# Prompt attention of a hybrid decoder step: a third PSUM bank for the transposes of the probabilities, and the next head's preparation emitted one step earlier with its factor chain in two parts

## The chip, the cores and the metric

One core of a Trainium2 chip runs the whole program. TensorE (PE) multiplies and transposes into PSUM, which has eight banks of 512 fp32 columns; VectorE (DVE), ScalarE (ACT) and GpSimd (POOL) do the rest, and SyncE (SP) issues nearly all transfers. The metric is the device time of one execution in microseconds, the median of several runs; lower is better.

## The reference, cut to what matters

One inference step of a two-layer decoder for a prompt of 1024 tokens and eight samples. Layer 1 is multi-head latent attention with eight heads; the change touches only its prompt half:

```
def mla_attend_prompt(q_abs, q_pe, ckv, kpe, ks):
    for qb in range(t // Q_BLOCK):                      # 8 blocks of 128 queries
        lo, hi = qb * Q_BLOCK, (qb + 1) * Q_BLOCK
        s = mla_scores(q_abs[:, lo:hi], q_pe[:, lo:hi], ckv[:, :hi], kpe[:, :hi], ks[:, :hi])
        p = jax.nn.softmax(jnp.where(mask[None, None], s, -jnp.inf), axis=-1)
        outs.append(jnp.einsum('bhqk,bkc->bqhc', p.astype(ckv.dtype), ckv[:, :hi]))
...
    ms = (sum(k_nope ** 2) + sum(kpe_raw ** 2)) / QK_HEAD
    kscale = lax.rsqrt(ms + EPS)                        # one factor per key and head
    qn = rms_norm(q, q_g)                               # one factor per query and head
```

## The kernel before

The program is a chain of stages; most of its 2 ms go to the projections, the samples' attention over a paged cache and the two output projections. The prompt's attention, `mla()`, begins when all earlier stages have been emitted and is followed by the output projection `out1()`. fp32 products are made of three matmuls on split operands (`mm3`, lines 189 to 191), of a high part H and a low part L.

`mla()` loops over eight heads `h` and in each over eight blocks `i` of 128 queries. One step (h, i) emits, in this order:

- `soft(h, i)`: scores (matmuls of lines 1421 to 1427 into one or two banks of the pool `mm`, which has three), a multiply with a running maximum on DVE (`ass`, line 1429), the negated maximum (`anb`, 1432), the exponential on ACT (1434), the reciprocal of its sum on DVE (`als`, 1435);
- in even heads from 2 on, at i = 2 to 5, one tile of the values for two heads (`vals`, 12 matmuls of 256 columns, here called a values tile);
- one part of the generator `prep(h + 1)`, which prepares the next head: two halves of the keys (k c0, k c1), two of the queries (q c0, q c1), the sums of squares (`ast`, line 1366, copied by DVE to `asts`, 1368), their transposes (line 1372) with the factor chain on DVE (lines 1376 to 1379, where `rsqrt_` makes ten small instructions on 128x16 elements), and last the transpose `tk` (1382) and the stores and loads of the key factor;
- `step(h, i - 2)`: the transposes of the probabilities of two blocks earlier (`tr`, line 1453, tile `atp`, one bank for up to four 128x128 transposes), then, after each second block, the product with the values (`pvl`, tile `aO`), then the split of the transposed probabilities into `aPTH` (ACT, line 183) and `aPTL` (DVE, line 179), which frees the bank.

Of PSUM's eight banks `mm` has three, tag `s` two, and tags `x`, `v` and `t` one each. `atp` rotates through the two of `s`; `ast`, `ast2` and `tk` use `v`, `aO` uses `t`; `x` serves stages before `mla()` and is not used in it.

All engines run their instructions in order. The order on each engine follows the program, but the layer below moves instructions of one engine past each other where it reckons that they would wait, so the emitted order is read from the listing of each engine.

`prep` is advanced once before the loop over i and once in each step:

```
g0 = prep(0)
for _ in range(5):
    next(g0)
...
for h in range(8):
    nxt = prep(h + 1) if h < 7 else iter(())
    ...
    next(nxt, None)
    for i in range(8):
        ss, ls = soft(h, i)
        ...
        next(nxt, None)
```

Of the kernel before, what the change touches and what calls it, by code (L numbers as in the profile page):

```python
# [5 lines left out]
F = mybir.dt.float32  # L6
R = mybir.dt.float32r
I32 = mybir.dt.int32
# [4 lines left out]
ALU = mybir.AluOpType  # L13
# [79 lines left out]
def build(nc, tc, I, O):  # L93
    A, V, G, T, S = nc.scalar, nc.vector, nc.gpsimd, nc.tensor, nc.sync
# [38 lines left out]
    def mmt(name="mm"):  # L133
        return psm.tile([128, 512], F, tag="mm", name=name)

    def pst(tag, name):
        return psx.tile([128, 512], F, tag=tag, name=name, bufs=2 if tag == "s" else 1)
# [55 lines left out]
    cnt = [0]  # L193
    sm = {}

    def rsqrt_(p, out, v, shape):

        cnt[0] += 1
        t = p.tile(shape, F, tag="rsq", name=f"rsq{cnt[0]}")
        P = shape[0]  # L200
        t, out, v = t[0:P], out, v
        V.tensor_scalar(out=out.bitcast(I32), in0=v.bitcast(I32), scalar1=-0.5, scalar2=float(0x5F3759DF), op0=ALU.mult, op1=ALU.add)
        for _ in range(3):
            V.tensor_tensor(out=t, in0=out, in1=out, op=ALU.mult)
            V.scalar_tensor_tensor(out=t, in0=t, scalar=-0.5, in1=v, op0=ALU.mult, op1=ALU.mult)
            V.scalar_tensor_tensor(out=out, in0=t, scalar=1.5, in1=out, op0=ALU.add, op1=ALU.mult)

    def stat_r(p, sqs, tiles, n, tag, eps=EPS, keep=None):

        nt = len(tiles)  # L210
        ps = pst("x", "stat" + tag)
        for i, (c0, m) in enumerate(tiles):
            for j, sq in enumerate(sqs):
                T.matmul(ps[0:m, 2 * i:2 * i + 2], sq[:, c0:c0 + m], ones[:, 0:2], start=(j == 0), stop=(j == len(sqs) - 1))
        v = (keep or p).tile([128, nt], F, name="stv" + tag, tag="stv" + (tag if keep else ""))
        r = (keep or p).tile([128, nt], F, name="str" + tag, tag="str" + (tag if keep else ""))
        if tiles[-1][1] < 128:
            V.memset(v, 1.0)
        for i0, i1, m in ([(0, nt, 128)] if tiles[-1][1] == 128 else [(0, nt - 1, 128), (nt - 1, nt, tiles[-1][1])]):
            V.tensor_scalar(out=v[0:m, i0:i1], in0=ps[0:m, 2 * i0:2 * i1].rearrange("p (i two) -> p i two", two=2)[:, :, 0], scalar1=1.0 / n, scalar2=eps, op0=ALU.mult, op1=ALU.add)  # L220
        rsqrt_(p, r, v, [128, nt])
        return v, r
# [112 lines left out]
    def mem_kv(side=None):  # L335
# [32 lines left out]
        for l in range(2):  # L368
# [5 lines left out]
            for u in range(4):  # L374
# [17 lines left out]
                if u == 1:  # L392
                    v = pp.tile([128, 8], F, name="ksv", tag="ksv")
                    r = pp.tile([128, 8], F, name="ksr", tag="ksr")
                    xv = pp.tile([128, 8], F, name="kxv", tag="kxv")
                    for m in range(2):
                        V.tensor_scalar(out=xv[:, 4 * m:4 * m + 4], in0=sm["memn"][0][:, m:m + 1].broadcast_to([128, 4]), scalar1=EPS, scalar2=None, op0=ALU.mult)
                    V.scalar_tensor_tensor(out=v, in0=ssq, scalar=1.0 / 128, in1=xv, op0=ALU.mult, op1=ALU.add)
                    rsqrt_(pp, r, v, [128, 8])
                    for m in range(2):  # L400
                        for h in range(4):
                            V.scalar_tensor_tensor(out=kn[m][:, h, :], in0=kn[m][:, h, :], scalar=r[:, 4 * m + h:4 * m + h + 1], in1=gk, op0=ALU.mult, op1=ALU.mult)
                        S.dma_start(out=O["mk"][l, m * 128:(m + 1) * 128, :], in_=kn[m].rearrange("p h d -> p (h d)"))
                    if l == 0:
                        xn = halves()
                        for k in range(8):
                            scaled(1, xn, k)
# [901 lines left out]
    def mla():  # L1309
# [3 lines left out]
        p = LP.new("ma_")  # L1313
# [16 lines left out]
        def prep(h):  # L1330
# [7 lines left out]
            qp = p.tile([128, NP], R, name="aqp", tag=f"aqp{h % 2}")  # L1338
            qr = p.tile([128, NP], F, name="aqr", tag="aqr")
            S.dma_start(out=qr[0:64], in_=d_qp[h // 2, 64 * (h % 2):64 * (h % 2) + 64, :])  # L1340
            yield 0.5
            for c in range(2):
                ps = mmt()
                fm(ps, 512, w, 2, ckH, ckL, c * 512)
# [11 lines left out]
            for c in range(2):  # L1356
                ps = mmt()
# [16 lines left out]
            v = p.tile([128, 16], F, name="akv", tag="akv")  # L1374
            rs = p.tile([128, 16], F, name="aks", tag="aks")
            V.tensor_tensor(out=v.rearrange("p (j c) -> p j c", j=4), in0=st, in1=ssq[:, :, h].rearrange("p (j c) -> p j c", j=4), op=ALU.add)
            V.tensor_tensor(out=v, in0=v, in1=fac, op=ALU.mult)
            V.tensor_scalar(out=v, in0=v, scalar1=EPS, scalar2=None, op0=ALU.add)
            rsqrt_(p, rs, v, [128, 16])
            yield 1.0  # L1380
            tk = pst("v", "tk")
            T.transpose(tk[0:8, 0:128], rs[:, 0:8], ident)
            kt = p.tile([8, 128], F, name="akt", tag="akt")
# [58 lines left out]
            else:  # L1442
                V.tensor_scalar(out=ss[:, 0:kv], in0=ss[:, 0:kv], scalar1=ls, scalar2=None, op0=ALU.mult)

        PTs = {}

        def tr(i, ss):
            out = []
            for b0 in range(0, i + 1, 4):
                nb = min(4, i + 1 - b0)  # L1450
                ps = pst("s", "atp")
                for b in range(nb):
                    T.transpose(ps[:, b * 128:(b + 1) * 128], ss[:, (b0 + b) * 128:(b0 + b + 1) * 128], ident)  # L1453
                out.append((b0, nb, ps))
            return out
# [13 lines left out]
        def pvl(h, i, H, L):  # L1469
# [15 lines left out]
            end()  # L1485
# [4 lines that stand above are left out]
# [462 lines left out]
```

## Time and profile before

| | |
|---|---|
| median of three runs | 2034.68 us (2033.48 to 2039.29) |
| the profiled execution | 2020.94 us, span 2019.1 us |
| PE busy | 1919.3 us, 95% of the span |
| DVE, ACT, POOL busy | 990.9, 744.9, 665.0 us |
| mean granted clock of PE | 0.98 of full speed |
| `mla()`, from its first head's preparation to its last product | about 1562 to 1875 us of the span |

The runs are timed without the profiler; the profiled execution is one of its own. Its time is the span plus 1.84 us. In the lists of idle time, each gap of an engine is put down to the instruction that released it.

### The profile page before, as it was taken

To read this page: it belongs to the slowest core of one execution; us is meant where nothing else is said; L and a number is where in the kernel's file an instruction comes from. 1 tells how busy PE (TensorE), PEld (TensorE's weight loads), DVE (VectorE), ACT (ScalarE), POOL (GpSimd) and SP (SyncE) were. 2 spreads that over 40 slices of the span, in tenths; PEclk is the share of its full clock that TensorE was granted. 3 is DMA by queue.
4 is the path that set the end of the run, shared out by engine and by line. 5 is a ranking of instruction groups with operands and counts; after the bars stand their busy time and mean duration, and the time that the engine had idled before them with its cause. 6 is when DMAs were issued, how large, how long until landed. Compare 5 with 4: busy or idle time off the path is not lost. (4 is left out here: it accounts for less than half of the span.)

```text
span 2019.1 us, 35721 instructions
## 1 busy us (share of the span) xinstructions
PE 1919.3 (95%) x12508; PEld 1655.5 (82%) x12508; DVE 990.9 (49%) x2578; ACT 744.9 (37%) x1499; POOL 665.0 (33%) x588
## 2 busy tenths in 40 slices
PE   6987999998999999999999999999998899998999
PEld 6987998988997877777788776777787687787999
DVE  7559454456653534444323444445456556657300
ACT  6434323333321133333222422333343666667300
POOL 4544432422220213333333334332322333432220
PEclk8999999989999999999999999999999999999999
DMA  6553535552446378787998888887852211113532
GB/s 223 169 193 91 176 98 211 146 158 87 154 142 217 101 242 284 226 293 250 313 322 286 268 278 293 265 258 247 283 169 69 84 57 58 65 43 129 183 95 73
DMA packets 192884, 368.28 MB, mean 182 GB/s; under 512 B 27809, under 2 KB 135585, under 8 KB 191426
## 3 DMA queue, kind: packets, MB, share of 16 engines
q1 hardware_dynamic: 172178, 298.75, 45.2%
q0 software_dynamic: 20528, 67.26, 10.4%
q8 instruction: 99, 1.62, 0.3%
q14 instruction: 79, 0.65, 0.1%
HBM read 331.22 MB, written 34.70 MB: 181 GB/s over the span
## 5 line engine op out<-in xcount | busy, mean ns | idle before, releaser
L1078 POOL DMA_INDIRECT nat<-nat,IX x256 | 271.6, 1061 | 490.1 <-PE pv L1163 422.6
L189 PE MATMUL mm<-xH,whi 128*128 128x384 f32 (+1 forms) x1112 | 372.7, 335 | 10.6 <-ACT whi L183 5.9
L191 PE MATMUL mm<-xH,wli 128*128 128x384 f32 (+1 forms) x1112 | 367.2, 331 | 6.6 <-POOL wli L179 4.1
L190 PE MATMUL mm<-xL,whi 128*128 128x384 f32 (+1 forms) x1112 | 367.1, 330 | 0.3 <-DVE xL L179 0.3
L189 PEld LDWEIGHTS mm<-xH,whi 128*128 128x128 f32 x1112 | 214.2, 193 | 27.4 <-issue 10.3
L183 ACT ACTIVATE whi<-wri 128x1024 fp32r<-128x1024 f32 (+1 forms) x130 | 126.3, 978 | 265.9 <-PE mm L190 202.3
L191 PEld LDWEIGHTS mm<-xH,wli 128*128 128x128 f32 x1112 | 213.7, 192 | 8.6 <-POOL wli L179 4.9
L190 PEld LDWEIGHTS mm<-xL,whi 128*128 128x128 f32 x1112 | 213.7, 192 | 3.9 <-issue 2.8
L179 POOL TENSOR_TENSOR wli<-wri,whi 128x1024 fp32r<-128x1024 f32 (+1 forms) x65 | 146.7, 2261 | 163.3 <-ACT whi L183 158.1
L1092 PE MATMUL sAB<-rec,qar 128*64 128x256 f32 x1024 | 149.5, 389 | 0.0
L1163 PE MATMUL pv<-nat,PT 128*64 128x256 f32 x1024 | 139.5, 394 | 7.8 <-ACT PT L1143 6.3
L1163 PEld LDWEIGHTS pv<-nat,PT 128*64 128x64 f32 x1024 | 76.3, 139 | 51.0 <-ACT PT L1143 14.3
L1092 PEld LDWEIGHTS sAB<-rec,qar 128*64 128x64 f32 x1024 | 79.5, 138 | 42.6 <-issue 11.5
L179 DVE TENSOR_TENSOR wli<-wri,whi 128x1024 fp32r<-128x1024 f32 (+1 forms) x65 | 73.7, 1136 | 80.3 <-ACT whi L183 79.4
L1107 DVE CUSTOM_DVE_ANT_1 ss<-sAB,rec,mx 128x256 f32<-128x256 f32 x120 | 57.9, 483 | 101.6 <-PE sAB L1097 90.4
L189 PE MATMUL mm<-nH,whi 128*128 128x384 f32 x304 | 104.8, 345 | 0.6 <-ACT whi L183 0.6
L190 PE MATMUL mm<-nL,whi 128*128 128x384 f32 x304 | 102.7, 338 | 0.8 <-DVE nL L240 0.8
L191 PE MATMUL mm<-nH,wli 128*128 128x384 f32 x304 | 102.2, 336 | 0.0
L179 POOL TENSOR_TENSOR wlo<-wro,who 128x768 fp32r<-128x768 f32 (+3 forms) x30 | 59.0, 1975 | 120.4 <-ACT who L183 120.4
L189 PE MATMUL mm<-yHo,who 128*128 128x384 f32 (+1 forms) x288 | 96.9, 337 | 0.9 <-ACT yHo L183 0.9
L191 PE MATMUL mm<-yHo,wlo 128*128 128x384 f32 (+1 forms) x288 | 94.5, 328 | 0.4 <-DVE wlo L179 0.4
L190 PE MATMUL mm<-yLo,who 128*128 128x384 f32 (+1 forms) x288 | 94.0, 326 | 0.4 <-DVE yLo L179 0.4
(594 smaller groups left out, 4335.9 us busy)
## 6 DMA issues: line engine op xcount, KB each, us to landing
rec<-rec SPq DMA_DIRECT2D x512, 192.0 KB
wri<-wi SPq DMA_DIRECT2D x114, 512.0 KB
wro<-wo SPq DMA_DIRECT2D x29, 384.0 KB
smkv<-ckm SPq DMA_DIRECT2D x16, 512.0 KB
smkv<-cvm SPq DMA_DIRECT2D x16, 512.0 KB
wrm<-memw SPq DMA_DIRECT2D x7, 1024.0 KB
wro<-wo SPq DMA_DIRECT2D x7, 768.0 KB
yld<-d_ys SPq DMA_DIRECT2D x8, 544.0 KB
```

The lines of the kernel that those rows point to most:

```text
L179: eng.tensor_tensor(out=out, in0=a, in1=h.bitcast(F), op=ALU.subtract)
L183: A.activation(h, src, AF.Copy)
L189: T.matmul(out, wh, xh, start=first, stop=False)
L190: T.matmul(out, wh, xl, start=False, stop=False)
L191: T.matmul(out, wl, xh, start=False, stop=last)
L1078: G.indirect_dma_start(out=t[:, j % 2, :], out_offset=None, in_=I["nat"], in_offset=bass.IndirectOffsetOnAxis(ap=IX[:, q:q + 1], axis=0), ...
L1092: T.matmul(s[x][64 * ab:64 * ab + 64, 0:256], QA[:, cb, b, :], part(t, cb * 128 + ab * 64)[:, 4 * x:4 * x + 4, :], start=(cb == 0), stop=F ...
L1107: V.tensor_tensor_reduce(out=ss[:, 256 * x:256 * x + 256].rearrange("p (g k) -> p g k", g=4), in0=s[x][:, 0:256].rearrange("p (g k) -> p g ...
L1163: T.matmul(d["v"][64 * ab:64 * ab + 64, 0:256], PT[:, j, ab, :], n[j][:, ab * 256:ab * 256 + 256], start=(i == 0 and j == 0), stop=(i == C ...
```

## The change

The changed kernel takes the banks of `atp` from `s`, `s`, `x` in turn, so that three banks rotate. `rsqrt_steps` is `rsqrt_` as a generator that yields after the first and the third of its three iterations, and `prep` no longer yields after its first DMA. `prep` so has eight parts as before, but each part up to the sums of squares is emitted one step earlier, and the factor chain, until now one part at i = 5, is emitted at i = 4 (transposes, first iteration) and i = 5 (second and third). Nothing else is changed, and no instruction is added or removed in what `mla()` computes.

```
+    def rsqrt_steps(p, out, v, shape):
+        cnt[0] += 1
+        t = p.tile(shape, F, tag="rsq", name=f"rsq{cnt[0]}")
+        V.tensor_scalar(out=out.bitcast(I32), in0=v.bitcast(I32), scalar1=-0.5, scalar2=float(0x5F3759DF), op0=ALU.mult, op1=ALU.add)
+        for n in range(3):
+            V.tensor_tensor(out=t, in0=out, in1=out, op=ALU.mult)
+            V.scalar_tensor_tensor(out=t, in0=t, scalar=-0.5, in1=v, op0=ALU.mult, op1=ALU.mult)
+            V.scalar_tensor_tensor(out=out, in0=t, scalar=1.5, in1=out, op0=ALU.add, op1=ALU.mult)
+            if n != 1:
+                yield
...
             S.dma_start(out=qr[0:64], in_=d_qp[h // 2, 64 * (h % 2):64 * (h % 2) + 64, :])
-            yield 0.5
             for c in range(2):
...
-            rsqrt_(p, rs, v, [128, 16])
-            yield 1.0
+            for _ in rsqrt_steps(p, rs, v, [128, 16]):
+                yield 0.5
...
-        PTs = {}
+        PTs, ntr = {}, [0]
...
-                ps = pst("s", "atp")
+                ps = pst("ssx"[ntr[0] % 3], "atp")
+                ntr[0] += 1
```

On DVE, in an even head, the factor chain of the kernel before, from its seed (line 202) to the split of the transposed probabilities of i = 3 (`aPTL`, four blocks); `[waits X]` says which engines' semaphores an instruction waits for:

```order
L202 TENSOR_SCALAR aks<-akv 128x16 [waits DVE_49]
L204 TENSOR_TENSOR rsq_22046<-aks 128x16 [waits DVE_49]
L205 SCALAR_TENSOR_TENSOR rsq_22046<-rsq_22046,akv 128x16 [waits DVE_49]
L206 SCALAR_TENSOR_TENSOR aks<-rsq_22046,aks 128x16 [waits DVE_49]
L204 TENSOR_TENSOR rsq_22046<-aks 128x16 [waits DVE_49]
L205 SCALAR_TENSOR_TENSOR rsq_22046<-rsq_22046,akv 128x16 [waits DVE_49]
L1429 ISA ass,amx<-mm,akb 128x512 [waits PE_49]
L1429 ISA amx 128x1
L206 SCALAR_TENSOR_TENSOR aks<-rsq_22046,aks 128x16 [waits DVE_49]
L179 TENSOR_TENSOR aPTL<-atp,aPTH 128x4x128 [waits Activation_49]
```

In the changed kernel (its lines are 11 or 12 higher; 212 to 216 are `rsqrt_steps`) the same chain stands in front of the split of i = 2 (three blocks) and the scores of i = 5:

```order
L212 TENSOR_SCALAR aks<-akv 128x16 [waits DVE_49]
L214 TENSOR_TENSOR rsq_21986<-aks 128x16 [waits DVE_49]
L215 SCALAR_TENSOR_TENSOR rsq_21986<-rsq_21986,akv 128x16 [waits DVE_49]
L216 SCALAR_TENSOR_TENSOR aks<-rsq_21986,aks 128x16 [waits DVE_49]
L214 TENSOR_TENSOR rsq_21986<-aks 128x16 [waits DVE_49]
L1492 SCALAR_TENSOR_TENSOR as_21886<-as_21886,aO 128x256 [waits DMAHW6_49,DMAHW0_49,PE_49]
L215 SCALAR_TENSOR_TENSOR rsq_21986<-rsq_21986,akv 128x16 [waits DVE_49]
L179 TENSOR_TENSOR aPTL<-atp,aPTH 128x3x128 [waits Activation_49]
L216 SCALAR_TENSOR_TENSOR aks<-rsq_21986,aks 128x16 [waits DVE_49]
L1440 ISA ass,amx<-mm,akb 128x512 [waits PE_49]
```

The chain has moved up by one block: what comes behind it is now the split of i = 2 and the scores of i = 5, where it was the split of i = 3 and the scores of i = 6.

On PE, the transposes of i = 4 (five blocks, so two banks) in the kernel before, with the product with the values behind them:

```order
L1453 MATMUL atp<-ident,ass 128x128 [waits Activation_49]
L1453 MATMUL atp<-ident,ass 128x128 x3
L189 MATMUL aO<-aPTH,avH 128x256 [waits Activation_49]
L1421 MATMUL mm<-akH,aqH 128x512 [waits PE_49]
L1453 MATMUL atp<-ident,ass 128x128 [waits DVE_49,PE_49]
L190 MATMUL aO<-aPTL,avH 128x256
```

In the changed kernel:

```order
L1393 MATMUL tk<-ident,aks 8x128 [waits DVE_49]
L1465 MATMUL atp<-ident,ass 128x128 [waits Activation_49]
L1465 MATMUL atp<-ident,ass 128x128 x4
L189 MATMUL aO<-aPTH,avH 128x256 [waits Activation_49]
L190 MATMUL aO<-aPTL,avH 128x256 [waits DVE_49]
```

The fifth transpose no longer waits for DVE, and `tk`, which stood behind it, now stands ahead of all five.

On PE at the end of a head, the kernel before has the end of the scores of the next head's i = 0, k c0 of the head after it, and the transposes of i = 6:

```order
L1425 MATMUL mm<-kpL,aqp 128x128
L1427 LDWEIGHTS idb
L1427 MATMUL mm<-cmb,idb 128x128
L189 MATMUL mm<-ckH,whk 128x512 [waits DVE_49]
...
L191 MATMUL mm<-ckH,wlk 128x512
L1453 MATMUL atp<-ident,ass 128x128 [waits DVE_49]
L1453 MATMUL atp<-ident,ass 128x128 x3
L1453 MATMUL atp<-ident,ass 128x128 [waits DVE_49]
```

In the changed kernel k c0 comes ahead of these scores, and k c1 stands where k c0 stood:

```order
L189 MATMUL mm<-ckH,whk 128x512
...
L191 MATMUL mm<-ckH,wlk 128x512
L1432 MATMUL mm<-akH,aqH 128x128 [waits DVE_49]
...
L1438 MATMUL mm<-cmb,idb 128x128
L189 MATMUL mm<-ckH,whk 128x512 [waits DVE_49]
...
L1465 MATMUL atp<-ident,ass 128x128 [waits Activation_49]
L1465 MATMUL atp<-ident,ass 128x128 x3
L1465 MATMUL atp<-ident,ass 128x128 [waits DVE_49]
```

Each of the four matmul parts has moved up by one step; the transposes of i = 6 have their first wait on ACT instead of DVE.

## Rows read from the trace of the kernel before

**Rows 1.** The page: busy time of each engine (share of the span, instructions), and the clock granted to PE in 40 slices, in tenths of full speed.

```profile
PE 1919.3 (95%) x12508; PEld 1655.5 (82%) x12508; DVE 990.9 (49%) x2578; ACT 744.9 (37%) x1499; POOL 665.0 (33%) x588
PEclk8999999989999999999999999999999999999999
```

**Rows 2.** Who PE waited for: four stretches one after the other (1568 to 1590 us, the first head's preparation; 1590 to 1630; 1630 to 1840; 1840 to 1875, the end of the attention). Columns: total us, times, longest.

```profile
PE tk L1382 <- DVE aks L206: 2.6, 1, 2.6
PE ast L1366 <- ACT asq L1346: 0.8, 1, 0.8
PE mm L1424 <- POOL aqp L179: 0.7, 1, 0.7
...
PE tk L1382 <- DVE aks L206: 0.8, 1, 0.8
PE atp L1453 <- DVE aPTL L179: 0.8, 1, 0.8
...
PE atp L1453 <- DVE rsq L204: 9.9, 6, 3.0
PE atp L1453 <- DVE aPTL L179: 4.2, 5, 0.8
PE aO L189 <- ACT aPTH L183: 1.1, 4, 0.4
...
PE atp L1453 <- DVE aPTL L179: 2.5, 5, 1.0
```

**Rows 3.** Stretches of PE: length, busy time (x instructions), granted clock, DMA share, GB/s.

```profile
1578.80:1581.85 3.05, 3.05 (x10) 0.51 0.32 76
1680.80:1684.00 3.20, 3.20 (x13) 0.50 0.11 33
1756.50:1760.00 3.50, 3.19 (x21) 1.00 0.01 2
1680.30:1716.00 35.70, 33.92 (x209) 0.95 0.21 64
1757.00:1791.00 34.00, 32.22 (x209) 1.00 0.17 56
```

**Rows 4.** PE in order of time in the even head 2 (start us, duration, line, what, shape of one, count, [idle before <- releaser]); each row is the first instruction of a unit.

```profile
1668.38 1.06 PE L1366 MATMUL ast<-asq,ones 128*32 128x512 f32 x8
1669.38 0.55 PE L1453 MATMUL atp<-ident,ass 128*128 128x128 f32 x3
1669.68 0.36 PE L189 MATMUL aO<-aPTH,avH 128*128 128x256 f32 x1
...
1670.40 0.44 PE L1421 MATMUL mm<-akH,aqH 128*128 128x512 f32 x1
...
1672.24 0.36 PE L189 MATMUL mm<-whv,ckH 128*128 128x256 f32 x1
...
1673.76 0.60 PE L1372 MATMUL ast<-ident,asts 128*128 128x128 f32 x4
1674.19 0.60 PE L1453 MATMUL atp<-ident,ass 128*128 128x128 f32 x4
1674.55 0.48 PE L1421 MATMUL mm<-akH,aqH 128*128 128x512 f32 x1
...
1676.76 0.60 PE L1453 MATMUL atp<-ident,ass 128*128 128x128 f32 x4
...
1680.07 0.30 PE L1453 MATMUL atp<-ident,ass 128*128 128x128 f32 x1 [2.36 <-DVE rsq L204]
```

**Rows 5.** DVE in the same head: the start of the factor chain, its two longest instructions, the scores of i = 6 and the split of i = 3.

```profile
1674.39 0.18 DVE L1376 TENSOR_TENSOR akv<-ast,ssq 128x16 f32<-128x16 f32 x1 [0.94 <-PE ast L1372]
...
1676.04 1.16 DVE L206 SCALAR_TENSOR_TENSOR aks<-rsq,aks 128x16 f32<-128x16 f32 x1
1677.23 1.20 DVE L204 TENSOR_TENSOR rsq<-aks 128x16 f32<-128x16 f32 x1
...
1678.55 0.68 DVE L1429 CUSTOM_DVE_ANT_0 ass<-mm,akb 128x512 f32<-128x512 f32 x1
...
1679.24 0.68 DVE L179 TENSOR_TENSOR aPTL<-atp,aPTH 128x512 fp32r<-128x512 f32 x1
```

**Rows 6.** POOL in the same head: the last values tile split into H and L, then the next weights.

```profile
1675.15 0.61 POOL L1321 CAST avH<-araw 128x512 fp32r<-128x512 f32 x1 [2.77 <-ACT araw L1320]
1675.84 1.32 POOL L179 TENSOR_TENSOR avL<-araw,avH 128x512 fp32r<-128x512 f32 x1
1677.12 1.27 POOL L179 TENSOR_TENSOR wlv<-wrv,whv 128x512 fp32r<-128x512 f32 x1
```

**Rows 7.** The same chain in the odd head 1, where POOL has no values to split: DVE's first instruction of the chain and the split of i = 3, and PE's transpose behind them.

```profile
1635.78 0.17 DVE L1376 TENSOR_TENSOR akv<-ast,ssq 128x16 f32<-128x16 f32 x1
...
1638.25 0.68 DVE L179 TENSOR_TENSOR aPTL<-atp,aPTH 128x512 fp32r<-128x512 f32 x1
1639.08 0.30 PE L1453 MATMUL atp<-ident,ass 128*128 128x128 f32 x1 [0.72 <-DVE rsq L204]
```

**Rows 8.** The end of head 2: DVE's reciprocal for i = 7 and the second split of i = 5, and PE's transposes of i = 6.

```profile
1688.92 0.16 DVE L1435 RECIPROCAL als<-als 128x1 f32<-128x1 f32 x1 [0.80 <-ACT ass L1434]
1689.19 0.42 DVE L179 TENSOR_TENSOR aPTL<-atp,aPTH 128x256 fp32r<-128x256 f32 x1
1689.67 0.55 PE L1453 MATMUL atp<-ident,ass 128*128 128x128 f32 x3 [0.84 <-DVE aPTL L179]
```

## The prediction

> **What bounds the kernel now.** The page comes first: PE is busy for 1919.3 us of a span of 2019.1, DVE for half of it [rows 1]. So the kernel is bound by PE nearly everywhere, and what a change to the prompt's attention can give is the time in which PE stands still or runs slowly there. The change touches nothing before 1562 us or after 1875 us. In that stretch the list of who PE waited for gives, added up: 9.9 us in six waits of the transposes (`atp`) put down to `rsq`, 5.0 us (4.2 and 0.8) in six waits of the transposes for `aPTL`, 4.9 us in the first head's preparation and head 0 (2.6, 0.8, 0.7 and 0.8), 1.1 us for `aPTH`, and 2.5 us at the end [rows 2]. To this comes the clock: PE ran at half speed (0.50 and 0.51) in two pieces of about 3 us, after the waits of 2.6 and of 2.36 us; after another wait of the same place, at 1756, the granted clock stayed 1.00 [rows 3]. All of this together, with the 1.7 and 1.5 us that the clock costs (below), is 26.6 us, 1.3% of the run: more than that the change cannot give.
>
> Next, which resource each wait is for. In the even head 2, PE reaches the fifth transpose of i = 4 at 1677.71 and starts it at 1680.07 [rows 4]. That transpose begins a second bank, and with two banks in turn it needs the one that held i = 3. This is free when DVE has split it into `aPTL`, which ends at 1679.92 (1679.24 + 0.68) [rows 5]; the page's `rsq` is the instruction right behind. The split is late because the factor chain stands ahead of it on DVE: from its first instruction to the end of the split 5.53 us pass in the even head (1674.39 to 1679.92) and 3.15 in the odd head 1 (1635.78 to 1638.93), where the wait is 0.72 [rows 5, 7]. The difference of 2.4 us lies in instructions of 128x16 elements that last 1.16 and 1.20 us; the first ends at 1677.20, where POOL's `avL` ends (1677.16), and the second at 1678.43, where POOL's `wlv` ends (1678.39) [rows 5, 6]. So DVE's small instructions stand still while POOL works, and POOL has such work in even heads.
>
> The waits of 0.84 us at the end of a head are the same resource without the chain: the last three transposes of i = 6 start 0.06 us after the second split of i = 5, and this stood on DVE behind a reciprocal that waited for ACT's exponential of i = 7 [rows 8].
>
> **The change part by part.** No instruction goes or comes; the sum is made of waits.
>
> *The third bank at the end of a head.* The second bank of i = 6 now waits for the first split of i = 5, which stands ahead of that reciprocal. The k c0 part that PE runs before lies there as before, only another half of the keys. So the six waits of 0.8 go: 5.0 us [rows 2]. Bounds 2.5, if that first split should stand as late in some heads, and 5.0.
>
> *The chain in its new place, with three banks.* The fifth transpose of i = 4 now needs the split of i = 2. From the end of the transposes of line 1372 PE has ahead of it, by the starts in rows 4: three transposes 0.30, `aO` 0.72, scores of i = 5 1.84, a values tile 1.52, four transposes 0.36, scores of i = 6 2.21, together 6.95 us in an even head and 5.43 in an odd one, where it had 3.52 (1674.19 to 1677.71) [rows 4]. DVE needs at most the 5.53 and 3.15 us of before up to that split [rows 5, 7]. The wait at the transposes goes. What is late next is the scores of i = 5 on DVE, which stand behind the chain, and they free a bank of `mm`. With three such banks, in an even head the scores of i = 6 need it after 4.74 us (all but the last term above); DVE has read it 0.68 us behind the split, after 6.2 us if POOL holds it up as now and after 3.8 if not: a wait of 0 to 1.5 us. POOL's weights no longer fall on the chain, a values tile does (0.61 + 1.32 us instead of 3.2 in all) [rows 6], so I take 0.6. In an odd head only the second half of the scores of i = 6 needs the bank, after 4.5 us (1.26 of the 2.21 more, the values tile less), against 3.15 + 0.68 and some 0.2 for one more small instruction: 0, up to 0.7 if the scores of i = 4 in front of the chain make it start late; I take 0.3. Three heads of each kind: 2.7 us stay of 9.9, a gain of 7.2, with bounds 3.3 (6.6 stay) and 9.9.
>
> The Trainium skill, page "SBUF — State Buffer", section "Who interferes with whom", says that a VectorE instruction with two SBUF inputs is fully blocked by a GpSimd instruction that reads SBUF, and that who issues first decides. The 1.16 and 1.20 us agree. It speaks against the change: a chain in two parts is as long as one, and by that rule the whole 1.9 us of POOL's values tile would fall on it, 1.0 us of wait per even head instead of 0.6, so 14.8 us in place of the 16.0 below.
>
> *The clock.* The stretch with the slow piece lasts 35.7 us, the same work two heads later 34.0 [rows 3]: 1.7 us, which go with the wait of 2.36 that led to it; bounds 0 and 1.7.
>
> *The first head.* Its sums of squares move ahead of the first values tile, where nothing hides the last square on ACT, a loss of up to 1 us; in return the chain and `tk` come one values tile (1.52 us [rows 4]) earlier than the 2.6 us wait. All waits of this stretch are 4.9 us [rows 2], and its 3.05 us at half clock cost 1.5 [rows 3]. Bounds -1 and +6.4, and I take 1.3, nearer to the loss, since the chain is no shorter there.
>
> *The end.* Of the 2.5 us of waits for `aPTL` [rows 2] a part is for other things in front on ACT; bounds 0 and 2.5, taken 0.8.
>
> *What costs nothing.* k c0 of the next head ahead of the scores of i = 0 and the DMA issue without a part of its own: the PE work of a head is the same, and PE is the bound. The cover lost is in steps 3 to 6 of odd heads, where no matmul part stands any more; this is the slower rival below. The bank `x` has no other user here.
>
> Sum: 5.0 + 7.2 + 1.7 + 1.3 + 0.8 = 16.0 us. The profiled execution took 2020.94 us (its span and 1.84), 13.7 less than the median of the runs; taking the same difference, 2004.9 there and 2034.7 - 16.0 = 2018.7 us for the median. The bounds of the terms give 4.8 (3.3 + half of 5.0 + 0 - 1 + 0) and 25.5 us, so 2029.9 and 2009.2.
>
> **The rivals.**
>
> *The wait moves to the score banks.* The chain plus POOL's work holds the scores of i = 5 as long as it held the split: 1.5 and 0.7 us stay per head (6.6), the clock still falls now and then, first head and end give nothing. For: DVE's work in steps 4 and 5 of a head is the chain on top of everything else, and it stays in order. Against: PE's cover is twice as long as before. 3.3 + 5.0 = 8.3 us, 2026.4.
>
> *Everything goes.* No wait stays and the first head loses none: 25.5 us at most; some 22, 2012.7. Against: chain and scores are within 1 us of each other above.
>
> *The change does not do what it says.* PE's transposes may wait for DVE in its order whichever bank they get, so a third bank only renames the wait. Against: the 0.06 us of rows 8, and the listing, where the fifth transpose has lost its wait for DVE. Gain under 6 us, some 3, 2031.7.
>
> *Slower.* The place is line 1372 in odd heads: its transposes wait for DVE's copy of the sums of squares. Between the sums and these transposes PE had three transposes, `aO` and the scores of i = 5, 2.86 us without the values tile (1669.38 to 1672.24) [rows 4]; now it has two transposes and the scores of i = 4, some 1.7 us. The copy is one DVE instruction of 512 columns, 0.68 us as the others [rows 5], but behind the maximum and perhaps the reciprocal of i = 3, and a late copy delays the chain and the scores behind it as well. It decides once PE waits 2.3 us there in each of seven heads (16.0 / 7), so when the copy ends 4 us after the sums; at 3 us each the median would be 2034.7 - 16.0 + 21 = 2039.7. Against: 0.68 is far from 4.
>
> **How the numbers follow.** Forecast (11 to 21 us) 0.6; moved wait 0.18; everything goes 0.07; renamed 0.1; slower 0.05. 0.3% of the run, 6.1 us, is about what a measurement tells from no change. The first three are faster: 0.85; the fourth is within 0.3%: 0.1; slower 0.05. The range from 2010 to 2031 holds the first two, nearly all of the third and part of the fourth; the likeliest one's own is 2014 to 2024.
>
> **What would show it.** Right: no wait of `atp` on `rsq` or `aPTL` above 0.3 us between 1590 and 1830; small waits of score matmuls on `ass` in even heads; the granted clock 1.00 throughout the heads; an odd head near 33 us (34.0 [rows 3] less 0.8 and 0.4). Wrong: waits of 1 us or more at the score matmuls (moved wait), at line 1372 (slower), or `atp` still waiting for DVE (renamed); and a first head that has become longer.

## The result, and the profile after

The changed kernel takes 2017.17 us (median; 2013.66 to 2022.82) beside 2034.76 for the kernel before: 17.6 us less, a ratio of 0.9912 with a 95% interval of 0.9892 to 0.9932, which is 13.8 to 22.0 us. The forecast was 2018.7. Its profiled execution took 2015.58 us (2020.94 before).

The page of after, busy time and PE's granted clock, against [rows 1]:

```profile
span 2013.8 us, 35700 instructions
PE 1916.2 (95%) x12508; PEld 1652.8 (82%) x12508; DVE 985.0 (49%) x2578; ACT 742.0 (37%) x1499; POOL 663.8 (33%) x588
PEclk8998999989999999999999999999999999999999
```

The two spans differ by 5.3 us only, since the execution profiled before was a quick one ahead of the attention: its last transposes of `qpt` (the last PE work ahead of the first head's queries) start at 1560.29 us, those of after at 1575.24. In the other profiles below the same point lies between 1557 and 1586. So all profiles are compared from there to the end of the span, called the attention's length here (it includes the output projection): 2019.1 - 1560.3 = 458.8 us before, 2013.8 - 1575.2 = 438.6 after, **20.2 us less**, inside the interval of the timing.

Who PE waited for in after, in the stretches 1590 to 1630, 1630 to 1840 and 1840 to 1875, against [rows 2] (total us, times, longest):

```profile
PE tk L1393 <- DVE aks L216: 2.2, 1, 2.2
PE atp L1465 <- DVE aPTL L179: 0.4, 1, 0.4
...
PE atp L1465 <- DVE aPTL L179: 2.2, 5, 0.8
PE aO L190 <- DVE aPTL L179: 1.0, 3, 0.3
PE aO L189 <- ACT aPTH L183: 0.7, 1, 0.7
PE atp L1465 <- ACT ass L1452: 0.7, 1, 0.7
...
PE aO L190 <- DVE aPTL L179: 0.3, 1, 0.3
```

The waits for `rsq` are gone and so are nearly all of the 0.8 us at the ends of heads. The four largest that are left, 0.65 to 0.81 us, lie between 1831 and 1839 us, in the end of head 6; from 1636 to 1830 us all waits add up to 1.7 us. No wait is put down to the transposes of the sums of squares (line 1372, now 1383), and none of the score matmuls to `ass`.

A head's length is taken between DVE's last `as` (the reading of the last product) of one head and of the next. These are the windows of heads 2, 3 and 4 of before (length, PE busy, granted clock, DMA):

```profile
1660.21:1701.38 41.17, 37.97 (x244) 0.96 0.20 60
1701.38:1736.88 35.50, 33.72 (x220) 1.00 0.19 62
1736.88:1776.53 39.65, 36.39 (x244) 1.00 0.17 53
```

and of after:

```profile
1669.48:1706.71 37.23, 36.61 (x244) 1.00 0.22 68
1706.71:1739.77 33.06, 32.90 (x220) 1.00 0.21 66
1739.77:1777.00 37.23, 36.61 (x244) 1.00 0.19 56
```

An odd head is 2.4 us shorter, an even one 2.4, and head 2 another 1.5 for its piece at half clock, which did not come back. The rest: the stretch up to the end of head 0 went from 64.4 to 61.2 us, heads 6 and 7 together from 64.0 to 60.6.

### The profile page after: what moved, and what is told of

Its sections match the earlier page's. It is cut to its first block, busy times and chain, and to the rows that moved or that the text cites. A ratio compares the mean times of both kernels' runs of the same rounds, so it can differ in the third digit from the quotient of the medians.

```text
span 2013.8 us, 35700 instructions
## 1 busy us (share of the span) xinstructions
PE 1916.2 (95%) x12508; PEld 1652.8 (82%) x12508; DVE 985.0 (49%) x2578; ACT 742.0 (37%) x1499; POOL 663.8 (33%) x588
```

## Experiments

Twelve runs; "before" and "after" are the two kernels above. Four of them ran on two other chips (e_pause on one, the three on the first head on the other), on which the kernel before itself took 2017.5 and 2016.9 us, so medians are compared by their ratio to it. Lengths are of one profiled execution each, in us:

| kernel | third bank | parts a step earlier | pause ahead of `tk` | chain cut | attention | head 3 | head 4 | ratio of times (95%) |
|---|---|---|---|---|---|---|---|---|
| before | | | | | 458.8 | 35.50 | 39.65 | |
| e_bank | yes | | | | 451.4 | 34.28 | 38.48 | 0.9977 (0.9960 to 0.9994) |
| e_unshift | yes | | yes | yes | 456.7 | 36.77 | 39.57 | 1.0013 (0.9995 to 1.0032) |
| e_shift | | yes | | | 445.9 | 33.74 | 37.60 | 0.9937 (0.9913 to 0.9961) |
| e_pause | | yes | yes | | 442.7 | 33.82 | 37.60 | 0.9928 (0.9903 to 0.9952) |
| e_prep | | yes | yes | yes | 442.0 | 33.49 | 37.60 | 0.9920 (0.9894 to 0.9945) |
| e_whole | yes | yes | yes | | 438.4 | 33.37 | 37.26 | 0.9920 (0.9901 to 0.9940) |
| after | yes | yes | yes | yes | 438.6 | 33.06 | 37.23 | 0.9912 (0.9892 to 0.9932) |

The intervals of the times of e_shift, e_pause, e_prep, e_whole and after overlap, so only the traces tell these five apart. There the pieces in which PE ran at half speed (granted clock 0.50) blur differences of 1 to 2 us: before has one in the first head and one in head 2, e_bank and e_unshift have a third in head 6, e_shift has them in the first head and head 7, e_pause in the first head and head 6, e_prep in the first head alone, e_whole and after have none. Such a piece cost 1.5 us in head 2 of before and 1.6 in the first head of e_v4dve (below). Heads 3 and 4 ran at a granted clock of 1.00 in all eight.

### The third bank alone (e_bank)

```
-        PTs = {}
+        PTs, ntr = {}, [0]
-                ps = pst("s", "atp")
+                ps = pst("ssx"[ntr[0] % 3], "atp")
+                ntr[0] += 1
```

> The kernel before with the third bank alone; the next head's parts stand as before. Measure: attention's length, from the last `qpt` transposes to the end of the span: 458.8 us before, 438.6 after the whole change (20.2 less); medians 2034.8 and 2017.2. Theory A (bank and early chain need each other): the six 0.8 us waits at the end of the heads go, but the waits of i = 4 behind the factor chain only move from the fifth transpose to the product aO of i = 3, which needs the same split (`aPTL` of i = 3, still behind the chain on DVE): 9.9 us become 8 to 10. Attention some 451 to 454, median 2027 to 2030, waits of aO on aPTL or rsq of 0.5 us (odd heads) and 2 us (even heads). Rival B (the bank does nearly all): attention under 443, median under 2021. Rival C (the early chain does nearly all): attention over 456, median over 2032.

Attention 451.4 us, ratio 0.9977: theory A. PE in head 4 at i = 4 (start, duration, line, what, count, [idle before]):

```profile
1764.68 0.71 PE L1454 MATMUL atp<-ident,ass 128*128 128x128 f32 x5
1765.15 0.36 PE L189 MATMUL aO<-aPTH,avH 128*128 128x256 f32 x1
1767.97 0.39 PE L190 MATMUL aO<-aPTL,avH 128*128 128x256 f32 x1 [2.45 <-DVE aPTL L179]
```

The five transposes run through, as rows 4 did not, and the second matmul of `aO` waits 2.45 us for the same split. Between 1616 and 1845 us `aO` waits 8.6 us in six waits, where the transposes had waited 9.9 for `rsq`: the bank alone renames that wait. What it gains over heads 1 to 5, 6.0 us, are the waits at the ends of heads.

### Early parts and cut, with two banks (e_prep)

The diff of the change without the three lines above.

> The changed kernel with two banks for the transposes as before: the next head's parts stand one step earlier and the factor chain is emitted in two parts, nothing else. Theory A: the split of i = 3 stands behind one half of the chain only, so the six long waits of the fifth transpose shrink (2.4 us to about 0.9 in even heads, 0.7 to 0.3 in odd ones), the half-speed pieces go, but the 0.8 us waits at the end of a head stay: attention 446 to 450 us (of 458.8 and 438.6), median 2025 to 2029. Rival B (the bank does nearly all): attention over 454. Rival C (the early chain does nearly all): attention under 442, median under 2020, and no wait of 0.8 at the end of a head.

Attention 442.0 us, 16.8 less than before, between theory A and rival C and nearer to C. From 1612 to 1833 us PE waited for:

```profile
PE atp L1464 <- DVE aPTL L179: 7.2, 10, 1.7
```

In heads 1 to 5 these are waits for a bank: in each head for the first one of i = 5 (0.56 to 0.62 us), in even heads also for the second one of i = 4 (0.76 us). Over the heads 1 to 5 an even head is 37.60 us and an odd one near 33.5, 0.4 more than in after. The 0.8 us at the ends of heads are gone without a third bank. The reason is in PE's order. Before, PE ran `k` c0 of the next head ahead of the last three transposes of i = 6, and c1 behind the product; now c0 stands ahead of the scores of (h+1, 0) and c1 behind them, 1.46 us more PE work ahead of the transposes that need the bank. So the early parts cover the same wait that the third bank removes.

### The chain in one piece, all else as in the change (e_whole)

```
-            for _ in rsqrt_steps(p, rs, v, [128, 16]):
-                yield 0.5
+            rsqrt_(p, rs, v, [128, 16])
+            yield 0.5
+            yield 0.5
```

> The changed kernel with the factor chain in one piece: third bank, parts one step earlier, all instructions of the chain at the first of its two places. Theory: what counts is that the chain starts a step earlier and that the transposes need the split before the last; the cut in two only shares the delay between two steps. The scores of i = 4 or 5 and the split behind the chain are up to 1.2 us later in even heads, which three banks of `mm` and of the transposes cover: attention within 3 us of 438.6, median 2016 to 2020. Rival (the cut carries the gain): the wait comes back at aO or at the scores, 1 us or more in each of seven heads, attention 446 or more, median 2024 or more.

438.4 us against 438.6: the cut of the chain is worth nothing here.

### The parts at their old place, bank and cut kept (e_unshift)

```
             S.dma_start(out=qr[0:64], in_=d_qp[h // 2, 64 * (h % 2):64 * (h % 2) + 64, :])
+            yield 0.5
```

> The changed kernel with the pause behind the DMA of the position half put back: third bank and chain in two parts, but every part one step later, so that the second half of the chain stands in step 6 and `tk` with the three DMAs behind it in step 7. Theory: the row of key factors (`akb`), which in the changed kernel is issued about 6 us before the next head's first scores read it, is issued some 4 us later and arrives after them: DVE waits 2 to 4 us for the DMA at i = 0 of each of seven heads, the three score banks fill, and PE loses about 2 us a head: attention near 452 us, median near 2031. Rival (only the bank and the cut count, the place does not): no such wait, attention within 3 us of 438.6.

456.7 us and a ratio of 1.0013: nearly the whole gain is lost to one line, 18.1 us against after where 13 were expected. DVE's wait for the row of key factors, and PE's two largest waits, both from head 1 on (total, times, longest):

```profile
DVE ass L1441 <- DMA akb<-d_ks: 10.7, 6, 3.4
```

```profile
PE aO L190 <- DVE aPTL L179: 8.2, 6, 2.4
PE atp L1466 <- DVE anb L1444: 5.0, 4, 2.3
```

The row arrives 1.8 us too late per head on average, as expected in kind, and the wait of i = 4 for the split stands as in e_bank. The cut with `tk` a step later costs 5.3 us against e_bank, and the late row is what the trace shows for it.

### The early parts alone (e_shift)

```
             S.dma_start(out=qr[0:64], in_=d_qp[h // 2, 64 * (h % 2):64 * (h % 2) + 64, :])
-            yield 0.5
```

> The kernel before with one line less: the pause behind the DMA of the position half is gone, so every part of the next head stands one step earlier; two banks, and the factor chain in one piece. Theory D, formed from the four runs so far (attention 458.8 us before, 438.6 after, 451.4 with the bank alone, 442.0 with early parts and the cut, 438.4 with bank and early parts without the cut): the place of the parts alone carries about 17 of the 20 us, the cut nothing. Attention 441 to 444 us, median 2014 to 2020, an odd head 33.4 to 33.8, an even one near 37.6, no wait of 0.8 at the end of a head. Rival (with two banks the cut is needed, since the split behind a whole chain comes late for the fifth transpose): attention 448 or more, waits of the transposes of 1 us or more at i = 4 or 5 in each head.

445.9 us, 12.9 of the 20.2 for one line less, between theory D and its rival. From 1612 to 1840 us PE waited for:

```profile
PE tk L1381 <- DVE aks L206: 7.3, 7, 1.4
PE atp L1452 <- DVE aPTL L179: 0.3, 2, 0.2
```

The transposes hardly wait, as theory D has it. But `tk`, one step behind the start of the chain, now comes up while DVE is still in it and takes the wait. The difference to e_prep is 3.9 us, 2.6 of them in heads 6 and 7 (63.7 against 61.1).

### One pause more ahead of `tk` (e_pause)

```
             rsqrt_(p, rs, v, [128, 16])
-            yield 1.0
+            yield 0.5
+            yield 0.5
```

> The kernel with the early parts alone (two banks, the chain in one piece; attention 445.9 us), and one pause more between the chain and `tk`, so that `tk` stands where the changed kernel has it; the chain is not cut. It is the kernel with early parts and cut (442.0) but for the cut. In the kernel with the early parts alone PE waits 9.6 us in eight waits for `tk`. Theory (of the cut only the place of `tk` counts): those waits of 1.2 us go, attention 440.5 to 443. Rival (with two banks the cut itself is needed): the wait goes from `tk` to the transposes or to aO behind the uncut chain, attention 445 or more.

442.7 us: the waits for `tk` are gone after the first head, and the cut adds 0.7 at most. So "emitted in two parts" works by the pause that it brings, `tk` a step later, and not by the cut. The rival has a part, though: the transposes now wait 7.7 us in ten waits, heads 1 to 5 are as long as in e_shift within 0.3 each, and of the 3.2 us gained 2.1 are in heads 6 and 7. With two banks the wait only changes its name in the earlier heads; what it shows as there is 7.3 to 7.7 us whichever name it has. Along this path the 20.2 us are 12.9 (early parts), 3.2 (pause), 0.7 (cut) and 3.4 (bank); with the bank first it takes 7.4, because both remove the waits at the ends of heads. The 0.7 and the 3.4 are no firmer than one half-speed piece, which e_pause has in head 6 and e_prep has not, and which e_prep has in the first head and after has not. Over heads 1 to 5, where the clocks of each pair are alike, the bank gives 6.0 us first and 2.1 last. That the pause and not the cut works is shown with two banks here and with three by e_whole, which keeps the pause.

### The chain twice as long (e_dbl_before, e_dbl_after)

```
+        for _ in range(3):
+            V.tensor_tensor(out=t, in0=out, in1=out, op=ALU.mult)
+            V.scalar_tensor_tensor(out=t, in0=t, scalar=-0.5, in1=v, op0=ALU.mult, op1=ALU.mult)
+            V.scalar_tensor_tensor(out=out, in0=t, scalar=1.5, in1=out, op0=ALU.add, op1=ALU.mult)
```

in before behind `rsqrt_`, and in after as three more rounds inside `rsqrt_steps`, with the pauses behind rounds two and six.

> The kernel before with twice as many Newton rounds in the factor chain (nine more instructions of 128x16 elements, by the trace some 0.21 us each from start to start, 1.9 us per head; the factors stay the same but for rounding). It measures how much delay of DVE the place of the chain covers. Theory: PE already waits for what stands behind the chain, so every head pays it in full: 7 or 8 times 1.9, attention 472 to 474 us (of 458.8). Rival (the waits are not due to the chain's length): under 463.

> The changed kernel with the same nine instructions more (three in the first part of the chain, six in the second). Theory: in its new place, with three banks, an odd head has nearly as much cover as the chain needs, an even head a little too little, so a part of the 1.9 us is hidden: some 0.5 to 1 us per odd head, 1 to 1.5 per even one, attention 444 to 448 us (of 438.6). Rival 1 (no cover was gained, the waits went for another reason): 451 or more. Rival 2 (ample cover): under 441.

469.9 us (11.1 more) and 449.5 (10.9 more), ratios 1.0049 (1.0032 to 1.0066) and 0.9957 (0.9936 to 0.9977). By the totals the theory for before and rival 1 for after look near; by heads neither theory holds. Before, a head with a chain 1.9 us longer is not 1.9 longer: head 3 gains 0.94, head 2 0.24, head 5 0.16, and head 4 1.79 with a piece at half clock (0.96 over the head) that it had not had. In after an odd head is 0.8 longer (33.86), an even one not at all:

```profile
1678.23:1715.49 37.26, 36.45 (x244) 1.00 0.21 67
1715.49:1749.35 33.86, 32.82 (x220) 1.00 0.20 65
```

The reason is DVE's order: the nine extra instructions stand behind the split that PE waits for, and not ahead of it. From the first instruction of the chain to the split of i = 3 it is 4.85 us in head 2 of before (1674.39 to 1679.24, [rows 5]) and 4.85 in head 2 of e_dbl_before (1704.67 to 1709.52), the other heads from 1 to 5 agree as closely in both pairs of kernels, and PE's wait there is the 2.36 us of rows 4 again:

```profile
1710.35 0.45 PE L1463 MATMUL atp<-ident,ass 128*128 128x128 f32 x1 [2.36 <-DVE rsq L204]
```

In after nearly all of the cost, 8.8 us, is in the first head, where the wait for `tk` grows from 2.2 to 3.9 and the clock falls to half (0.67 over 1590 to 1600). So this pair did not measure the cover it was made for, and what a chain longer ahead of the split would cost is not shown.

### POOL's values tile away from the chain (e_v4dve)

```
-VSP = "vggg"
+VSP = "vgvg"
```

> The changed kernel with one letter other: the third of the four values tiles of an even head, which falls beside the factor chain, is split by ACT and DVE (as the first tile is) and not by POOL. In the changed kernel's trace a chain instruction of line 215 lasts 1.15 us instead of 0.17 and one of line 212 0.47 while POOL's `avL` of this tile runs (1748.06 to 1750.06), and an even head is 37.23 us, 1.3 more than its work. Theory: POOL's reading of SBUF holds DVE up; without it these instructions last 0.17 to 0.2, DVE pays one split of 0.7 instead of 1.3 of standing still, and an even head falls by 0.3 to 1 us: attention 436 to 438. Rival (the instructions are late for another reason, or the split of 0.7 falls in a worse place): the same two lines stay long, or attention is 439 to 441.

436.6 us, ratio 0.9878 (0.9842 to 0.9915). Both even heads are 1.1 us shorter (36.15 and 36.17), odd ones the same within 0.4. DVE in head 4 of after (line 212, line 215, and the negated maximum of i = 5), with POOL beside it:

```profile
1748.24 0.47 DVE L212 TENSOR_SCALAR aks<-akv 128x16 int32<-128x16 int32 x1
...
1748.94 1.15 DVE L215 SCALAR_TENSOR_TENSOR rsq<-rsq,akv 128x16 f32<-128x16 f32 x1
...
1752.79 0.16 DVE L1443 SCALAR_TENSOR_TENSOR anb<-amx,arq 128x1 f32<-128x1 f32 x1
```

```profile
1748.06 0.62 POOL L1333 CAST avH<-araw 128x512 fp32r<-128x512 f32 x1 [2.54 <-ACT araw L1332]
1748.75 1.31 POOL L179 TENSOR_TENSOR avL<-araw,avH 128x512 fp32r<-128x512 f32 x1
```

and the same three instructions in e_v4dve, where POOL rests and DVE has one split of 0.69 more:

```profile
1749.68 0.17 DVE L212 TENSOR_SCALAR aks<-akv 128x16 int32<-128x16 int32 x1
...
1750.34 0.17 DVE L215 SCALAR_TENSOR_TENSOR rsq<-rsq,akv 128x16 f32<-128x16 f32 x1
...
1752.34 0.16 DVE L1443 SCALAR_TENSOR_TENSOR anb<-amx,arq 128x1 f32<-128x1 f32 x1
```

The two long instructions end where POOL's end (1748.71 and 1748.68; 1750.09 and 1750.06), and without POOL they last 0.17. From the first instruction of the chain to the negated maximum it is 5.16 us in after (1747.63 to 1752.79) and 4.08 in e_v4dve (1748.26 to 1752.34): 1.08 less, and the head is 1.08 shorter (37.23 to 36.15). Three things add up to it: the two instructions no longer stand still (1.28 less), the split with the wait for it costs DVE 0.81, and DVE's order has three instructions of the chain fewer ahead of the negated maximum (0.61 less). So POOL standing in DVE's way is shown to cost DVE 1.28 us in an even head, and the edit to give 1.08; what it would give with DVE's order unchanged is not shown. It reaches PE through `anb` and ACT: by PE's starts, counted from the beginning of head 4, after lags e_v4dve by 0.13 us at the scores of i = 6, 0.32 at the first matmul of `aO`, 0.95 two matmuls later, and 1.08 from the transposes of i = 5 on. ACT's exponential of i = 5 stands ahead of the split `aPTH` of i = 3 in ACT's order, `aPTL` follows it, and `aO` waits. In head 4 of after, ACT, DVE and PE:

```profile
1752.99 1.03 ACT L1445 ACTIVATE ass<-ass,anb,arq 128x768 f32<-128x768 f32 x1 [3.90 <-DVE anb L1443]
...
1754.49 0.58 ACT L183 ACTIVATE aPTH<-atp 128x512 fp32r<-128x512 f32 x1
```

```profile
1755.11 0.69 DVE L179 TENSOR_TENSOR aPTL<-atp,aPTH 128x512 fp32r<-128x512 f32 x1 [0.80 <-ACT aPTH L183]
```

```profile
1755.13 0.38 PE L189 MATMUL aO<-aPTH,avH 128*128 128x256 f32 x1
1755.85 0.39 PE L190 MATMUL aO<-aPTL,avH 128*128 128x256 f32 x1 [0.34 <-DVE aPTL L179]
```

The Trainium skill, page "SBUF — State Buffer", section "Who interferes with whom", states that a VectorE instruction with two SBUF inputs contends with a GpSimd instruction that reads SBUF, and that issue order decides who blocks. The 1.15 us of line 215, which has two such inputs and started behind POOL's instruction, agree, against 0.17 without it.

### The first head (e_qp0, e_both, e_first4)

```
-                sub(G, qp[64:128, q], qr[0:64, q], qp[0:64, q])
+                sub(V if h == 0 else G, qp[64:128, q], qr[0:64, q], qp[0:64, q])
```

> The changed kernel with the two `aqp` subtractions of the first head on DVE and not on POOL. In the changed kernel's trace PE waits 2.23 us for the factors (`tk`) in the first head, while two chain instructions of DVE last 1.17 and 1.19 us beside POOL's `aqp` (1589.35, 2.51 us). Theory: without POOL there these two last 0.2, DVE pays some 0.9 to 1.4 for the subtractions instead, the wait falls to 1 to 1.6 us, and the first stretch (from the last `qpt` to the last product of head 0) from 61.2 to 60.0 to 60.7. Rival (the subtractions wait for the late row `aqr` at the head of DVE's queue and hold the chain up): the wait is 2.5 or more, the stretch 61.5 or more.

Attention 439.6 us, ratio 0.9890 (0.9863 to 0.9918). The wait for `tk` falls to 1.24 us, but only because PE reaches `tk` later, with the values tiles done: `tk` starts 18.4 us behind the last `qpt`, in after 17.2. The two subtractions take 1.29 us of DVE (0.31 of waiting in front) and hold up what stands behind them; the row `akb` then holds DVE 9.0 us (5.4 in after), and a score matmul waits 1.11 us. The stretch is 62.7 us against 61.2, at a granted clock of 1.00 in both: no gain, so the theory has the wait right and its rival the stretch.

> The changed kernel with both edits: the third values tile of an even head is split by ACT and DVE, and the first head's `aqp` subtractions run on DVE. Theory: they act at different places and add up: even heads 36.15 as with the first edit alone (37.23 before it), the first stretch as with the second alone; attention 434 to 436.5 us (of 438.6), median 2010 to 2016, faster than the changed kernel by 2 to 5 us. Rival (PE's half-speed piece in the first head comes back whatever is done there, some 1.5 us): attention 436 to 438.

This kernel has both edits above. Attention 437.3 us, ratio 0.9887 (0.9867 to 0.9907); even heads 36.17 and 36.15, as expected, first stretch 63.0. The two edits do act at different places, but the one in the first head is a loss (63.0 and 62.7 against 61.2), so the sum of the theory is missed. The total lies in the rival's range without the rival's reason: the granted clock of the first head is 1.00 here.

```
-VSP = "vggg"
+VSP = "vgvg"
...
-        for _ in range(5):
+        for _ in range(4):
             next(g0)
```

> The changed kernel with the values tile split by ACT and DVE, and in the first head the sums of squares one place later, behind the first values tile, as in the kernel before (the prediction's loss of up to 1 us there, against its gain for `tk`). In the changed kernel these sums last 1.98 us instead of 1.0, waiting for ACT's last square. Theory: that 1.0 us comes back, and the wait for `tk` grows from 2.23 us by less than the 1.53 us of a values tile, since the chain is then clear of a part of POOL's work: the first stretch within 0.6 us of 61.2 (62.8 where the clock falls to half for a piece). Rival (`tk` is late by the whole tile): its wait 3.5 us or more and the stretch 62 or more at full clock.

Attention 438.8 us, ratio 0.9888 (0.9862 to 0.9913). The sums of squares and `tk` in the first head of after:

```profile
1582.41 2.05 PE L1377 MATMUL ast<-asq,ones 128*32 128x512 f32 x8
...
1592.45 0.27 PE L1393 MATMUL tk<-ident,aks 128*8 128x128 f32 x1 [2.23 <-DVE aks L216]
```

and of e_first4, with two windows of PE behind `tk` (length, busy, granted clock):

```profile
1565.25 1.07 PE L1377 MATMUL ast<-asq,ones 128*32 128x512 f32 x8
...
1575.00 0.37 PE L1393 MATMUL tk<-ident,aks 128*8 128x128 f32 x1 [2.82 <-DVE aks L216]
```

```profile
1572.65:1576.65 4.00, 1.65 (x7) 0.73 0.20 67
1576.65:1580.65 4.00, 4.00 (x15) 0.50 0.62 181
```

The 1.0 us at the sums comes back and the wait grows by 0.6, as the theory has it; but PE then runs at half speed for a piece (0.50), and the stretch is 64.5 us, beyond both of the theory's values and 1.7 more than with the values tile alone (e_v4dve), which had such a piece too, half as long.

No version here is faster than the changed kernel beyond the uncertainty of its times. By the traces e_v4dve is: 3.5 us less over heads 1 to 7 (230.7 against 234.1), of which a half-speed piece in its first head took back 1.6.

## Why the prediction was right, and where its working was not

The forecast of 16.0 us less met 17.6, and the direction and main mechanism hold: waits went, no work did. By places the sum misses more than its total. Put together by heads, its terms give 3.8 us for the three odd heads (0.72 - 0.3 + 0.84 each), 7.0 for heads 2 and 4 with the clock, 3.2 for heads 6 and 7, 2.1 up to the end of head 0. Measured: 7.4, 6.4, 3.4 and 3.2, in all 20.4 up to the last product (20.2 with the output projection). So against the traces the sum is 4 us short, 3.6 of them in the odd heads; that it comes within 1.6 us of the timing, whose interval is 13.8 to 22.0 us, is in part luck.

**The waits of 0.8 us at the end of a head (taken 5.0).** They go, and the bank alone takes them away (e_bank). But "what costs nothing: `k` c0 of the next head ahead of the scores of i = 0" was the step that failed: it is not neutral, it lies in front of the same transposes and covers the same wait without any bank (e_shift). The price was also too low. PE in head 3 of before, at that wait:

```profile
1722.27 0.66 PE L1453 MATMUL atp<-ident,ass 128*128 128x128 f32 x4
1723.77 0.55 PE L1453 MATMUL atp<-ident,ass 128*128 128x128 f32 x3 [0.84 <-DVE aPTL L179]
```

From start to start it is 1.50 us; four transposes without a wait take 0.36 ([rows 4], 1674.19 to 1674.55). So 1.14 us are lost, while the idle column shows 0.84: the 0.30 between counts as busy, because a matmul's modelled end lies behind the start of the next when nothing waits. This is the mis-sized term of the odd heads. Added by starts, head 3 of before loses 0.48 at the transposes of i = 4, 0.87 ahead of the fifth, 1.14 here and 0.17 at `k`, 2.7 us; the waits shown for it are 1.8.

**The chain in its new place (9.9 to 2.7).** The place is right and the part of the bank in it is not. The bank without the early parts moves 8.6 of the 9.9 us to `aO`; the early parts without the bank bring all waits of PE in the heads from 15.2 ([rows 2], third stretch) to 7.2 to 7.7 (e_shift, e_pause, e_prep), and the bank then to 1.7. The rest was forecast at the score banks, 0.6 in even and 0.3 in odd heads. From the first instruction of the chain to the end of the split it is 3.80 us in an even head now (1747.63 to 1751.43) and 3.19 in an odd one, where the prediction put at most 5.53 and 3.15. No score matmul waits for `ass`; what stays (1.7 us of waits from 1636 to 1830 us) is at `aO` and the transposes, and in an even head POOL's values tile is behind it: moving its split gave 1.08 us (e_v4dve). The weighing of the Trainium skill's rule named the right cause, 1.0 us for an even head, where the sum took 0.6; but it put the wait at the score banks, so the nearness of 1.0 and 1.08 is luck.

**The clock (1.7).** 1.5: head 2 was that much longer than head 4 before, and both are 37.23 now. The granted clock was 1.00 through all heads. It was not in every profile of the same form: with a wait for `tk` of 2.2 to 2.3 us, after and e_whole kept 1.00, e_shift, e_prep, e_pause and e_v4dve fell to 0.83 over the 10 us around it.

**The first head (1.3, bounds -1 and +6.4).** Measured 3.2 up to the end of head 0, of which the forecast had 2.1. The loss of 1 us at the sums came as put (from their start to that of the next unit 1.98 us, 1582.41 to 1584.39, and 1.00 before, 1568.88 to 1569.88), the wait for `tk` went from 2.6 to 2.2, and the waits for `aqp`, `tk` and `aPTL` of 0.7 to 0.8 are gone, as is the half-speed piece. That this piece stayed away cannot be put to the change: four other profiles with the same wait had it, e_whole had not, and in e_v4dve it cost 1.6 us.

**The end (0.8).** Not seen as a gain. By idle time, PE's waits behind the fifth transpose of head 6 and up to the last product add up to 3.2 us before and 3.3 after. Of the 3.4 us of heads 6 and 7, 2.7 are the wait of 3.03 us at that transpose (1832.56), which became one of 0.34 at `aO` (1826.10); the rest has no place. That the 3.2 forecast for these heads is near is luck, since this term of it did not come.

**The rivals.** The wait did not move to the score banks. "Renamed" is what the bank does alone to the wait of i = 4, and the early parts are why it did not decide. Nothing waits at line 1372. "Everything goes" (22 us) is nearer to the 20.2 of the traces than 16.0 is, and the interval of the times reaches to both; but waits remain, so it is not what happened.

## What to carry to other kernels

When a change has two parts that could each remove the same wait, price both alone: here the bank was worth 7.4 us first and 3.4 last (6.0 and 2.1 over heads 1 to 5), and one deleted pause carried most of the gain. Take the cost of a PE wait from the starts on both sides of it and not from the idle column. Before a run that lengthens a chain, look where the emitted order puts the added instructions. A small instruction that lasts a microsecond on DVE points to what POOL does beside it, and here moving that POOL work gave 1.08 us per even head, though PE never waited for POOL by name.

## What was not expected of the hardware

A DVE instruction with one input, `TENSOR_SCALAR` of 128x16, was held up as well: 0.47 us while POOL's CAST of `avH` ran, 0.17 in e_v4dve. And a half-speed piece of PE's clock followed a wait of 2.3 us in some profiles and not in others: after and e_v4dve have the same instructions in the same order up to head 2, and only the second had the piece, at a cost of 1.6 us in the first head (62.8 against 61.2). In before even a wait of 3.03 us, in head 6, left the granted clock at 1.00. Why is open.
